# Second MLP product: block sums kept unscaled in accumulators, and operands made for two feature pairs at once

## The chip, the cores and the metric

The kernel runs on one core of a Trainium2 chip. The core has TensorE (matrix products; PE in the profile, its weight loads PEld), VectorE (DVE), ScalarE (ACT), GpSimd (POOL), and SyncE (SP), which issues every transfer of this kernel. Products land in PSUM, everything else lies in SBUF; GpSimd's instructions here read and write SBUF alone. The metric is device microseconds of one execution, lower is better.

## The reference, cut to what matters

Two layers work on 128 context tokens and 1024 grid tokens of 1024 features. Each layer mixes tokens (not touched here) and then applies an MLP with 4096 hidden features:

```
h2 = rms_norm(x, norm2) * (1 + sc2) + sh2
x  = x + g2 * (square(relu(h2 @ w1)) @ w2)
```

`g2`, the gate, has one value per feature and condition; grid and context tokens have different conditions. After the first layer the next one norms x again and projects it; after the second, `rms_norm(x, norm_f)` is the output. The change concerns `@ w2`, the gate and the addition to x.

## The kernel before

**Layout.** Features lie on partitions, tokens along the free dimension: 1152 tokens, in three chunks of 384 for norms and projections, and in four blocks of 288 for the MLP. A block is a quarter of the grid tokens (256) and of the context tokens (32). `hd` in DRAM holds the squared hidden activations.

**Precision.** Each operand is split into two float32r parts: ScalarE rounds a copy (`acopy`, line 181), and a subtraction gives the rest, on GpSimd (`psub`, line 184) or VectorE (`vsub`, line 187). Each product is then three matmuls (lines 1081 to 1083).

**The second product.** Eight groups of four hidden tiles (512 features) follow each other; group g adds its part to all outputs. Within a group, for each of four pairs of output tiles (m) and each half of the tokens (q), a 2 by 2 product of blocks is done with seven products instead of eight (`Line.products`, line 1055 on). That is 4 x 2 x 7 x 2 x 3 = 336 matmuls of 288 columns a group. Such a set of seven for one m and q is called a line below. It ends in four blocks of sums in PSUM (bank names bA, bB, bC), plus a fifth product (bE) that is summed in `z` and added only in the last group.

**What VectorE does for it.** `second` takes each block out of PSUM: `x = gate * sums + x` (line 205), cut by `pieces` where a block crosses a chunk or changes condition: 2, 3, 2 and 2 pieces for the four blocks. x lies in SBUF for the whole product, loaded at its start by 24 transfers. `hidden_operands` (line 1218) makes the seven right operands for a pair of hidden tiles: four `vsub` of 288 columns in place (tile `xb`), seven rounded copies on ScalarE, and seven subtractions (tiles B and T), three on VectorE, four on GpSimd. It is called twice for each half of the tokens. `Weights` makes the left operands: per m and group four sums of 256 columns on VectorE (tile `wl`), seven rounded copies and seven subtractions (tile `wt`); `W2_SUBS` says how many of the seven are on VectorE (two for the first three m, then none).

**What sets the order.** A scheduler puts each engine's instructions in one order by priorities and its own costs, and pools of buffers add waits. The engines run their lists in that order. Within the last group, lines go by halves: all m for the first half of the tokens, then all m for the second. The norm of chunk 0 (`rms_sums`, `rms_rest`) and, in the first layer, its modulation for the next one (`modulate`) are written in between. After the last line come chunks 1 and 2. The next layer's first four projections (`xa`, `gel`) start from chunk 0.

Of the kernel before, what the change touches and what calls it, by code (L numbers as in the profile page):

```python
# [42 lines left out]
# a block of tokens: a quarter of the grid and one of the context  # L43
# [7 lines left out]
W1_SUBS, W2_SUBS = (2, 8, 2, 5), (2, 3)  # L51
# [47 lines left out]
def steps(n, span, i):  # L99
    """How many of n steps fall on i when they are spread over a span."""  # L100
# [17 lines left out]
def build(ctx, tc, I, O):  # L118
# [9 lines left out]
    def urgent(gen, offset):  # L128
        """A stream whose instructions go before those around it."""
# [7 lines left out]
    # pools that come and go  # L137
# [20 lines left out]
    def phase(st, tag, bufs, w=NW, side="left"):  # L158
        """A pool of [128, w] tiles for one phase of a layer."""
# [3 lines left out]
    def two_phases(st, tag, n1, n2, w):  # L163
        """The same in two places, by turns n1 and n2 tiles."""
# [72 lines left out]
    # the early columns apart from the others, which come later  # L237
# [18 lines left out]
    # adaLN vectors, feature on partitions: mod[l][:, j, cond]  # L256
# [3 lines left out]
    def mod_tile(l, j, piece):  # L260
        """mod[l][:, j] from the rows of w_mod's transpose, in pieces."""
# [19 lines left out]
    def segs(n):  # L281
        # (lo, hi, cond) within chunk n
# [4 lines left out]
    def rms_sums(xs, n, alone=False):  # L287
        """The sums over the feature tiles of the squares of chunk n."""
# [14 lines left out]
    def rms_scale(sq, ps, w=P):  # L303
        """1/rms of 3w tokens, to be turned."""
# [11 lines left out]
    def rms_turn(R, ps, w=P):  # L316
        """1/rms of 3w tokens on all partitions, in SBUF."""
# [16 lines left out]
    class HT:  # L334
        """Normalised and modulated activations in two float32r parts, [k][n]."""
# [49 lines left out]
    def weight(src):  # L385
        """The float32r parts of a [128, 8, 128] weight tile, as functions of its k."""
# [17 lines left out]
    def project_tokens(l, group, ht, evac, s_):  # L404
        """256 features projected with the tokens on partitions, 128 tokens a step."""
# [16 lines left out]
    def store_mix(t, dst, n, g_):  # L422
        """The float32r parts of a chunk of 128 features of the mixers' output, to DRAM."""
# [7 lines left out]
    class B:  # L431
        """The arrays of one pair of heads, in chunks of 384 tokens."""
# [243 lines left out]
    def hgrns(pairs):  # L676
        """Both pairs of heads: the end of each part runs under the levels of the next."""
# [10 lines left out]
    RG_STEPS = 1 + 2 * 7  # L688

    def rglru(l, i, xa, gel, gw, ud, g_):  # L690
# [13 lines left out]
        # each function of ScalarE for both directions at once  # L704
# [53 lines left out]
    def split_q(ps, n, h_t, l_t, sub):  # L758
        # queries in the order (row half, column block, row, column) and scaled
# [20 lines left out]
    def qk_project(l, p, win, ht, qd, kd, s_, ns=range(NCH)):  # L780
# [9 lines left out]
        def evac_k(n, ps):  # L790
            # the grid's rows in pairs, by columns
# [12 lines left out]
    # the grid's upper half for all pairs of heads, then the context's tokens and the lower half  # L804
# [4 lines left out]
    # where the output projection is done, by the tokens' half: of the first features, of the last  # L809
# [177 lines left out]
    class Ends:  # L987
        """What becomes of the fifth product and of the four blocks of a product of blocks."""
# [66 lines left out]
    class Line:  # L1055
        """Products of blocks one after the other, the end of each under the start of the next."""
# [53 lines left out]
    def pieces(b):  # L1110
        """Block b of tokens by chunks and conditions: (chunk, from, to, condition, place in the block)."""
# [4 lines left out]
    def half_of(q, t, d, load):  # L1116
        """Moves blocks 2q and 2q + 1 of a [128, 2 * BLK] tile from or to DRAM."""
# [5 lines left out]
    def pair_of(new, name):  # L1123
        return new(name, F32R).rearrange("p (j c) -> p j c", j=2)

    def parts(new, name, t, sub):
        o = pair_of(new, name)
        acopy(o[:, 0], t)
        sub(o[:, 1], t, o[:, 0])
        return o  # L1130

    def load_blocks(srcs, q, new):
        """Blocks 2q and 2q + 1 of two tiles of features."""
        x = []
        for s in srcs:
            t = new("xb")
            if t.shape[1] == 2 * BLK:
                dma(t, s[:, 2 * q * BLK:2 * (q + 1) * BLK])
                x.append((t[:, :BLK], t[:, BLK:]))
            else:  # L1140
                x.append((t[:, :BLK], new("xb")[:, :BLK]))
                for c in range(2):
                    dma(x[-1][c], s[:, (2 * q + c) * BLK:(2 * q + c + 1) * BLK])
        return x
# [22 lines left out]
    class NormOperands:  # L1167
        """The right operands of the seven products, from the features 2i and 2i + 1 of half q of the tokens.

        The steps take 2, 4, 4 and 4 places of [128, 2, BLK] (the second after the first, the fourth after the  # L1170
        others).
        """
# [12 lines left out]
        def normed(self, k):  # L1185
            """Normalised and modulated in place."""
# [31 lines left out]
    def hidden_operands(hd, g, q, i, new_x, new):  # L1218
        """The right operands of the seven products, from the hidden features 2i and 2i + 1 of group g."""
# [687 lines left out]
```

## Time and profile before

| | |
|---|---|
| times of three runs | 3359.71, 3369.78, 3373.78 us; median 3369.78 |
| the profiled execution | span 3359.0 us; its own time is not listed apart, the nearest run is 0.7 us above the span |
| busy shares of the span | PE 89%, PEld 84%, DVE 78%, POOL 52%, ACT 46% |
| second product, layer 0 | first matmul at 1293.7 us, last at 1745 us |
| second product, layer 1 | first matmul at 2886.5 us, last at 3329 us |
| after it, layer 1 | 30 us to the end of the span |

The profile's times are microseconds from the start of the span. A windows row gives, for a stretch, each engine's busy time and in brackets its instructions; then the mean clock that was granted to TensorE (1.00 is full speed), the busy share of the DMA engines and GB/s. A group row (lines) gives the line of the code, engine, operation, output and inputs by name, shape and count, then busy time and the mean nanoseconds of one instruction, then idle time before them and what ended it. Instructions on VectorE overlap a little: the next starts before the one before has written all, so the distance from start to start is shorter than the duration.

### The profile page before, as it was taken

To read this page: it belongs to the slowest core of one execution; us is meant where nothing else is said; L and a number is where in the kernel's file an instruction comes from. 1 tells how busy PE (TensorE), PEld (TensorE's weight loads), DVE (VectorE), ACT (ScalarE), POOL (GpSimd) and SP (SyncE) were. 2 spreads that over 40 slices of the span, in tenths; PEclk is the share of its full clock that TensorE was granted. 3 is DMA by queue.
4 is the path that set the end of the run, shared out by engine and by line. 5 is a ranking of instruction groups with operands and counts; after the bars stand their busy time and mean duration, and the time that the engine had idled before them with its cause. 6 is when DMAs were issued, how large, how long until landed. Compare 5 with 4: busy or idle time off the path is not lost. (4 is left out here: it accounts for less than half of the span.)

```text
span 3359.0 us, 62376 instructions
## 1 busy us (share of the span) xinstructions
PE 2987.9 (89%) x21196; PEld 2829.2 (84%) x21196; DVE 2627.3 (78%) x6417; ACT 1535.1 (46%) x3878; POOL 1735.7 (52%) x1822
## 2 busy tenths in 40 slices
PE   7888998898788888898878899999988999899885
PEld 7877987797788888898878789988878999888885
DVE  7799964678999998999996687345878324899997
ACT  5453234554432225554555533455635333555445
POOL 4541222444744437777765311334546555777776
PEclk8999999999899989999999999999989999999997
DMA  7332449973355555322232212689644333532222
GB/s 269 83 115 89 135 117 272 262 244 114 116 164 159 154 163 171 96 85 89 73 117 67 57 31 78 185 245 289 193 130 122 109 105 106 166 98 86 89 73 73
DMA packets 391070, 452.26 MB, mean 135 GB/s; under 512 B 68192, under 2 KB 293600, under 8 KB 390752
## 3 DMA queue, kind: packets, MB, share of 16 engines
q1 hardware_dynamic: 390752, 448.28, 44.5%
q8 instruction: 168, 2.75, 0.3%
q14 instruction: 150, 1.23, 0.1%
HBM read 339.34 MB, written 108.79 MB: 133 GB/s over the span
## 5 line engine op out<-in xcount | busy, mean ns | idle before, releaser
L184 POOL TENSOR_TENSOR wl<-wr,wh 128x512 fp32r<-128x512 f32 x164 | 226.8, 1388 | 476.6 <-ACT wh L181 380.2
L184 POOL TENSOR_TENSOR ws<-wl,ws 128x512 fp32r<-128x512 f32 x160 | 230.6, 1445 | 231.6 <-ACT ws L181 223.5
L1081 PE MATMUL bB<-t,ws 128*128 128x288 f32 x768 | 240.6, 313 | 73.0 <-DVE hr L193 68.3
L1081 PE MATMUL bB<-T,wt 128*128 128x288 f32 x768 | 240.8, 314 | 67.7 <-ACT bB L181 51.0
L184 POOL TENSOR_TENSOR wt<-wl,wt 128x256 fp32r<-128x256 f32 x296 | 253.0, 862 | 68.7 <-ACT wt L181 65.3
L392 PE MATMUL pj<-hh,wh 128*128 128x384 f32 x640 | 221.5, 351 | 21.4 <-DVE vb L178 7.3
L1082 PE MATMUL bB<-t,ws 128*128 128x288 f32 x768 | 236.3, 308 | 1.0 <-DVE t L187 1.0
L1083 PE MATMUL bB<-t,ws 128*128 128x288 f32 x768 | 236.6, 308 | 0.0
L270 DVE CUSTOM_DVE_ANT_0 junk<-wm,sil,ma 128x384 bf16<-128x384 f32 (+1 forms) x320 | 230.0, 719 | 6.7 <-DMA wm<-in_w_mod 1.9
L1082 PE MATMUL bB<-T,wt 128*128 128x288 f32 x768 | 233.9, 305 | 0.0
L1083 PE MATMUL bB<-T,wt 128*128 128x288 f32 x768 | 232.9, 303 | 0.0
L394 PE MATMUL pj<-hh,wl 128*128 128x384 f32 x640 | 222.4, 348 | 4.2 <-POOL wl L184 4.2
L393 PE MATMUL pj<-hh,wh 128*128 128x384 f32 x640 | 222.9, 349 | 3.4 <-DVE hh L205 3.4
L1081 PEld LDWEIGHTS bB<-t,ws 128*128 128x128 f32 x768 | 153.5, 200 | 81.1 <-DVE hr L193 74.8
L1081 PEld LDWEIGHTS bB<-T,wt 128*128 128x128 f32 x768 | 150.5, 196 | 82.0 <-ACT bB L181 60.6
L184 POOL TENSOR_TENSOR wt<-wr,wt 128x256 fp32r<-128x256 f32 x210 | 184.4, 881 | 60.8 <-ACT wt L181 52.2
L184 POOL TENSOR_TENSOR T<-xb,T 128x288 fp32r<-128x288 f32 x192 | 180.6, 950 | 42.7 <-ACT T L181 42.1
L187 DVE TENSOR_TENSOR xb<-xb 128x288 f32<-128x288 f32 x288 | 190.8, 667 | 11.5 <-POOL B L184 6.3
L181 ACT CAST ws<-wl 128x512 fp32r<-128x512 f32 x160 | 98.7, 620 | 194.8 <-PE bB L1083 91.2
L181 ACT CAST T<-xb 128x288 fp32r<-128x288 f32 x256 | 110.3, 432 | 165.8 <-DVE xb L187 147.3
L1081 PE MATMUL bA<-B,wt 128*128 128x288 f32 x512 | 158.6, 310 | 26.7 <-DVE x L205 23.7
L205 DVE SCALAR_TENSOR_TENSOR x<-bB,mod,x 128x256 f32<-128x256 f32 (+2 forms) x576 | 169.7, 339 | 12.5 <-PE bB L1083 11.5
(336 smaller groups left out, 11474.7 us busy)
## 6 DMA issues: line engine op xcount, KB each, us to landing
wr<-in_w SPq DMA_DIRECT2D x308, 256.0 KB, 3.0
hd<-hr SPq DMA_DIRECT2D x256, 144.0 KB, 2.6
wm<-in_w_mod SPq DMA_DIRECT2D x160, 192.0 KB, 2.7
wr<-in_w_in SPq DMA_DIRECT2D x104, 256.0 KB, 3.1
bi<-in_bias SPq DMA_DIRECT2D x96, 192.0 KB, 4.3
QS<-qd SPq DMA_DIRECT2D x72, 256.0 KB, 4.2
xb<-hd SPq DMA_DIRECT2D x128, 144.0 KB, 2.2
xb<-hd SPq DMA_DIRECT2D x64, 288.0 KB, 2.8
```

The costliest lines, as they stand in the source:

```text
L181: nc.scalar.copy(out=out, in_=in_)
L184: nc.gpsimd.tensor_tensor(out=out, in0=a, in1=b, op=ALU.subtract)
L187: nc.vector.tensor_tensor(out=out, in0=a, in1=b, op=ALU.subtract)
L205: nc.vector.scalar_tensor_tensor(out=out, in0=a, scalar=s, in1=b, op0=op0, op1=op1)
L270: nc.vector.tensor_tensor_reduce(out=junk[:, :w], in0=r[:, :w], in1=sil[:, c, k0:k0 + w], scale=1.0, scalar=acc[c], op0=ALU.mult, op1=ALU. ...
L392: mm(ps, lhsT=wh(k), rhs=ah(k), start=k == first, stop=False)
L393: mm(ps, lhsT=wh(k), rhs=al(k), start=False, stop=False)
L394: mm(ps, lhsT=wl(k), rhs=ah(k), start=False, stop=k == last)
L1081: mm(ps, lhsT=w[:, 0, ti(i)], rhs=t[:, 0], start=start and i == 0, stop=False, skip_group_check=True)
L1082: mm(ps, lhsT=w[:, 0, ti(i)], rhs=t[:, 1], start=False, stop=False, skip_group_check=True)
L1083: mm(ps, lhsT=w[:, 1, ti(i)], rhs=t[:, 0], start=False, stop=i == n - 1, skip_group_check=True)
```

## The change

1. The sums of a block go to an accumulator `acc` of 288 columns per block and output tile, without gate and without x. In group 0 ScalarE copies them out of PSUM; in the other seven, one VectorE addition per block. `z` is added to `acc` in the same way in the last group.
2. x is not loaded at the start. Where a chunk is complete, its eight x tiles are loaded (`load_chunk`) and `combine` does `x = gate * acc + x` on SBUF data: six pieces per output tile for all three chunks, 48 instructions a layer.
3. `hidden_operands` makes operands of both pairs at once: all its instructions are 576 columns wide, half as many. Its input tiles hold both pairs; there are two for all halves.
4. `W2_SUBS` becomes (4, 3, 2): four of seven subtractions of the left operands on VectorE for the first three m, then two.
5. At the end of layer 0, chunks 1 and 2 are loaded once the pools of the second product are closed, and both are modulated before the next layer's projections are written; before, chunk 2 was modulated after the projections of chunk 0.

Its core:

```diff
-W1_SUBS, W2_SUBS = (2, 8, 2, 5), (2, 3)
+W1_SUBS, W2_SUBS = (2, 8, 2, 5), (4, 3, 2)
+HIDDEN_SUBS = (0, 0, 1, 0, 0, 1, 1)
...
-    def hidden_operands(hd, g, q, i, new_x, new):
-        (a1, b1), (a2, b2) = load_blocks([hd[GRP * g + k] for k in (2 * i, 2 * i + 1)], q, new_x)
-        subs = iter((psub, psub, psub, vsub, psub, vsub, vsub))
+    def hidden_operands(hd, g, q, new_x, new):
+        src = hd[GRP * g:GRP * (g + 1)].rearrange("(i two) p t -> two p i t", two=2)
+        x = []
+        for s in range(2):
+            t = new_x("xb")
+            dma(t.rearrange("p (i t) -> p i t", i=2), src[s][:, :, 2 * q * BLK:2 * (q + 1) * BLK])
+            t = t.rearrange("p (i c m) -> p i c m", i=2, c=2)
+            x.append((t[:, :, 0], t[:, :, 1]))
+        (a1, b1), (a2, b2) = x
+        subs = iter(HIDDEN_SUBS)
+
+        def parts(name, t):
+            o = new(name, F32R).rearrange("p (j i m) -> p j i m", j=2, i=2)
+            acopy(o[:, 0], t)
+            (vsub if next(subs) else psub)(o[:, 1], t, o[:, 0])
+            return o
...
             def add(k, c, ps):
-                for n, a, b, cc, o in pieces(2 * q + c):
-                    t = xs[k][n][:, a:b]
-                    vstt(t, ps[:, o:o + b - a], mod[l][:, 40 + k, cc:cc + 1], t, ALU.mult, ALU.add)
+                t = acc[k][:, 2 * q + c]
+                if g == 0:
+                    acopy(t, ps)
+                else:
+                    vtt(t, ps, t, ALU.add)
...
+        def load_chunk(n):
+            for k in range(KD):
+                xs[k][n] = new_x("xo")
+                dma(xs[k][n], xmid[k][:, cs(n)])
+
+        def combine(n):
+            for k in range(KD):
+                t = xs[k][n]
+                g = mod[l][:, 40 + k]
+                for b in range(4):
+                    for nn, a, e, cc, o in pieces(b):
+                        if nn == n and cc == 0:
+                            vstt(t[:, a:e], acc[k][:, b, o:o + e - a], g[:, 0:1], t[:, a:e], ALU.mult, ALU.add)
+                if n == NCH - 1:
+                    u = t[:, NW - TP:].rearrange("p (b c) -> p b c", b=4)
+                    vstt(u, acc[k][:, :, BLG:], g[:, 1:2], u, ALU.mult, ALU.add)
...
             for n in range(NCH):
                 for m, e in first:
                     run_out(project(win(m), ht, e, (n,)))
-                if n == 0:
-                    modulate(l, False, xs, 2, ht)
```

**On VectorE, in the middle of layer 0's second product.** Twelve rows before (x is the residual, xb, B and T the right operands, wl the sums of weights):

```order
L187 TENSOR_TENSOR B_19406<-xb,B_19406 128x288
L193 TENSOR_TENSOR wl<-wr 128x256
L187 TENSOR_TENSOR xb<-xb 128x288
L187 TENSOR_TENSOR wl<-wl,wr 128x256
L187 TENSOR_TENSOR T_19416<-xb,T_19416 128x288
L205 SCALAR_TENSOR_TENSOR x_15501<-bA,mod_116,x_15501 128x256
L205 SCALAR_TENSOR_TENSOR x_15505<-bA,mod_116,x_15505 128x32
L205 SCALAR_TENSOR_TENSOR x_15503<-bA,mod_116,x_15503 128x256
L205 SCALAR_TENSOR_TENSOR x_15505<-bA,mod_116,x_15505 128x32
L205 SCALAR_TENSOR_TENSOR x_15507<-bB,mod_116,x_15507 128x128
L205 SCALAR_TENSOR_TENSOR x_15509<-bB,mod_116,x_15509 128x128
L205 SCALAR_TENSOR_TENSOR x_15511<-bB,mod_116,x_15511 128x32
```

and twelve after, from the same part of the product (acc is the accumulator, wt a part of a left operand):

```order
L188 TENSOR_TENSOR xb<-xb 128x2x288
L194 TENSOR_TENSOR acc<-bA,acc 128x288
L194 TENSOR_TENSOR z_16009<-bE,z_16009 128x288
L188 TENSOR_TENSOR xb<-xb 128x2x288
L194 TENSOR_TENSOR wl<-wr 128x256
L188 TENSOR_TENSOR wt<-wr,wt 128x256
L194 TENSOR_TENSOR acc<-bB,acc 128x288
L194 TENSOR_TENSOR acc<-bC,acc 128x288
L188 TENSOR_TENSOR wl<-wl,wr 128x256
L194 TENSOR_TENSOR acc<-bA,acc 128x288
L194 TENSOR_TENSOR acc<-bB,acc 128x288 x2
L188 TENSOR_TENSOR xb<-xb 128x2x288
```

Two or three instructions per block of sums have become one, the operands are twice as wide, and subtractions of weights (wt) now stand on VectorE.

**On ScalarE, where layer 1's first projections leave PSUM** (pj is the projection's bank, xa and gel its targets, sq squares for a norm, hh and hm modulated chunks). Before:

```order
L208 ACTIVATE hh_21185<-nt,mod_117 128x384
L208 ACTIVATE hh_21190<-nt,mod_117 128x384
L208 ACTIVATE sq<-x_15533 128x384
L181 CAST wh<-wr 128x512
L181 COPY xa<-pj 128x384
L181 CAST wh<-wr 128x512
L208 ACT_TABLE_LOAD
L208 ACTIVATE gel<-pj 128x384
```

After:

```order
L209 ACTIVATE hh_20657<-nt,mod_117 128x256
L209 ACTIVATE hh_20657<-nt,mod_117 128x128
L209 ACTIVATE hh_20665<-nt,mod_117 128x256
L209 ACTIVATE hh_20665<-nt,mod_117 128x128
L182 COPY xa<-pj 128x384 x2
L182 CAST wh<-wr 128x512 x2
L209 ACTIVATE gel<-pj 128x384
L182 CAST wh<-wr 128x512 x2
```

The first copy of `xa` stood between the norms of chunks 0 and 1; now it stands behind the last modulated tile of chunk 2 (hh_20665, in pieces of 256 and 128).

## Rows read from the trace of the kernel before

**Rows 1.** Windows: length, then busy us (xinstructions) of PE, PEld, DVE, ACT, POOL; PEclk, DMA.
```profile
1293.00:1340.00 47.00, 38.85 (x242) 35.67 (x243) 46.05 (x91) 27.16 (x81) 40.26 (x46) 0.93 0.65 210
1340.00:1653.00 313.00, 279.94 (x2003) 272.98 (x2003) 294.75 (x752) 157.62 (x437) 232.43 (x268) 0.97 0.29 88
1653.00:1745.00 92.00, 75.17 (x491) 71.92 (x489) 90.44 (x217) 47.30 (x118) 63.78 (x73) 0.93 0.28 95
1745.00:1800.00 55.00, 45.20 (x242) 43.17 (x241) 38.92 (x68) 30.44 (x64) 31.44 (x23) 0.91 0.29 96
2650.00:2850.00 200.00, 200.00 (x1510) 200.00 (x1510) 65.73 (x118) 72.32 (x156) 107.21 (x96) 1.00 0.34 103
```

**Rows 2.** Waits of TensorE, 1340 to 1653 us (total us, times, longest).
```profile
PE bB L1081 <- ACT bB L181: 21.9, 15, 4.0
```

**Rows 3.** VectorE's groups of instructions, 1340 to 1653 us (busy us, mean ns).
```profile
L187 DVE TENSOR_TENSOR xb<-xb 128x288 f32<-128x288 f32 x102 | 64.7, 639 | 4.2 <-POOL B L184 2.4 <-POOL T L184 1.7
L187 DVE TENSOR_TENSOR B<-xb,B 128x288 fp32r<-128x288 f32 x50 | 36.1, 732 | 2.5 <-ACT B L181 2.5
L187 DVE TENSOR_TENSOR T<-xb,T 128x288 fp32r<-128x288 f32 x25 | 14.5, 580 | 0.2 <-ACT T L181 0.2
L193 DVE TENSOR_TENSOR z<-bE,z 128x288 f32<-128x288 f32 x48 | 21.2, 445 | 0.3 <-PE bE L1083 0.3
L187 DVE TENSOR_TENSOR wl<-wr 128x256 f32<-128x256 f32 x24 | 18.8, 784 | 0.2
L187 DVE TENSOR_TENSOR wl<-wl,wr 128x256 f32<-128x256 f32 x23 | 13.8, 601 | 0.0
```

**Rows 4.** VectorE in order of time (start us, duration, line, instruction, count).
```profile
1665.47 0.63 DVE L205 SCALAR_TENSOR_TENSOR x<-bA,mod,x 128x256 f32<-128x256 f32 x2
1666.02 0.41 DVE L187 TENSOR_TENSOR wl<-wl,wr 128x256 f32<-128x256 f32 x1
1667.03 0.75 DVE L205 SCALAR_TENSOR_TENSOR x<-bC,mod,x 128x128 f32<-128x128 f32 x3
1667.70 0.44 DVE L187 TENSOR_TENSOR xb<-xb 128x288 f32<-128x288 f32 x1
1668.07 0.44 DVE L187 TENSOR_TENSOR B<-xb,B 128x288 fp32r<-128x288 f32 x1
...
1691.43 0.54 DVE L193 TENSOR_TENSOR sq<-sq 128x384 f32<-128x384 f32 x1
1691.89 0.41 DVE L187 TENSOR_TENSOR wl<-wr 128x256 f32<-128x256 f32 x1
```

**Rows 5.** VectorE while GpSimd works, in order of time.
```profile
1298.22 0.98 DVE L187 TENSOR_TENSOR T<-xb,T 128x288 fp32r<-128x288 f32 x1
1299.12 0.95 DVE L187 TENSOR_TENSOR wt<-wr,wt 128x256 fp32r<-128x256 f32 x1
1299.99 0.96 DVE L187 TENSOR_TENSOR wl<-wr 128x256 f32<-128x256 f32 x1
```

**Rows 6.** GpSimd in the same microseconds.
```profile
1297.94 1.85 POOL L184 TENSOR_TENSOR wt<-wl,wt 128x256 fp32r<-128x256 f32 x2
```

**Rows 7.** GpSimd's groups of instructions, 1340 to 1653 us.
```profile
L184 POOL TENSOR_TENSOR wt<-wl,wt 128x256 fp32r<-128x256 f32 x96 | 82.2, 861 | 27.5 <-ACT wt L181 27.4
L184 POOL TENSOR_TENSOR T<-xb,T 128x288 fp32r<-128x288 f32 x76 | 71.2, 946 | 14.0 <-ACT T L181 13.8
```

**Rows 8.** VectorE's groups of instructions, 1653 to 1745 us: the sums' last additions.
```profile
L205 DVE SCALAR_TENSOR_TENSOR x<-z,mod,x 128x32 f32<-128x32 f32 x16 | 10.6, 660 | 0.0
L205 DVE SCALAR_TENSOR_TENSOR x<-z,mod,x 128x128 f32<-128x128 f32 x16 | 9.8, 653 | 0.0
L205 DVE SCALAR_TENSOR_TENSOR x<-z,mod,x 128x256 f32<-128x256 f32 x8 | 5.9, 734 | 0.0
```

**Rows 9.** Waits of TensorE where layer 0 ends, 1720 to 1840 us.
```profile
PE pj L393 <- DVE hm L205: 4.8, 1, 4.8
```

**Rows 10.** VectorE's last instructions for the norm of the third chunk.
```profile
1788.84 2.06 DVE L205 SCALAR_TENSOR_TENSOR hh<-nt,mod,hh 128x256 fp32r<-128x256 f32 x6
```

More of the change, by code (lines that the diff above doesn't have):

```diff
@@ L1121, in half_of @@
             dma(*((a, d_) if load else (d_, a)))
[L1123 to L1144, printed above, removed]
     def blocks_of(t):
@@ L1704, in build @@
             sil_st.close()
-        x_st, h_st = ExitStack(), ExitStack()
-        X = x_st.enter_context(tc.tile_pool(name="x", bufs=24, side="right", reuse_waits="tile"))
-        st0, st1 = ExitStack(), ExitStack()
-        hr_ = phase(st0, "hr", 2, 2 * BLK, "right")
-        tp = [two_phases(st0, "tp0", 12, 2, 2 * BLK)]
+        h_st, acc_st, st0, st1, xs_st = (ExitStack() for _ in range(5))
+        acc_ = phase(acc_st, "acc", KD, T, "right")
+        hr_ = phase(st0, "hr", 2, 4 * BLK, "right")
+        tp = [two_phases(st0, "tp0", 6, 1, 4 * BLK)]
         ring2 = phase(st0, "wt", W2_RING, 4 * P, "right")
-        z_ = phase(st0, "z5", 8, BLK, "right")
-        tp += [two_phases(st1, "tp1", 11, 3, 2 * BLK), phase(st1, "tp2", 14, 2 * BLK, "right")]
+        z_ = phase(st0, "z5", 4, BLK, "right")
+        tp += [two_phases(st1, "tp1", 5, 2, 4 * BLK), phase(st1, "tp2", 7, 4 * BLK, "right")]
         def group_operands(s):
-            return [hidden_operands(hd, s // 2, s % 2, i, sqt if i % 2 else hr_, tp[s % 3]) for i in range(2)]
+            return hidden_operands(hd, s // 2, s % 2, hr_, tp[s % 3])
         ops = {s: group_operands(s) for s in range(2)}
-        xs = [[None] * NCH for _ in range(KD)]
-        for m in range(KD):
-            for n in range(NCH):
-                xs[m][n] = xt(f"x{m}")
-                dma(xs[m][n], xmid[m][:, cs(n)])
+        acc = [acc_("acc").rearrange("p (b m) -> p b m", b=4) for _ in range(KD)]
         z = [[None] * 2 for _ in range(KD // 2)]
@@ L1726, in build @@
         weights = Weights([I["w2"][l, g, m] for g in range(NG) for m, _ in order[g]], 2, lambda: ring2("wt", F32R), W2_RING,
-                          lambda i: lo_subs(W2_SUBS[0] if i < W2_SUBS[1] else 0))
+                          lambda i: lo_subs(W2_SUBS[0] if i < W2_SUBS[1] else W2_SUBS[2]))
         line = Line(banks, weights)
@@ L1746, in second @@
             return Ends(p5, *(lambda ps, r=r, c=c: add(2 * m + r, c, ps) for r in range(2) for c in range(2)))
-        def norm_part(n, k=KD):
-            pass
+        def load_chunk(n):
[13 more added lines that the diff above has]
+                    vstt(u, acc[k][:, :, BLG:], g[:, 1:2], u, ALU.mult, ALU.add)
         if not last:
             xold = tc.dram_tile([KD, P, T], F32, name=f"xd{l}")
+        xs = [[None] * NCH for _ in range(KD)]
         v = 0
@@ L1756, in build @@
                 for q in qs:
-                    line.add(v, q == qs[-1], lambda p, i, t=ops[2 * g + q]: t[i][p], 2, second(g, m, q))
+                    line.add(v, q == qs[-1], lambda p, i, t=ops[2 * g + q]: t[p][:, :, i], 2, second(g, m, q))
                     if g < NG - 1 and (m, q) in ((1, 1), (KD // 2 - 1, 1)):
@@ L1766, in build @@
                         ht = HT(8)
+                    new_x = phase(xs_st, "xo", (NCH if last else 1) * KD, NW, "right")
+                    load_chunk(0)
+                    combine(0)
                     sq = rms_sums(xs, 0)
@@ L1772, in build @@
                         finish(xs, 0, rs)
+                        for n in (1, 2):
+                            load_chunk(n)
                     else:
@@ L1777, in build @@
         line.end()
-        st0.close()
-        if last:
-            for n in (1, 2):
-                finish(xs, n, rms_chunk(xs, n, pa))
-            x_st.close()
-        else:
+        if not last:
+            xs_st.close()
+            st0.close()
+            new_x = phase(xs_st, "xo", 2 * KD, NW, "right")
+            with tc.high_priority(URGE2):
+                for n in (1, 2):
+                    load_chunk(n)
             ph = ExitStack()
             ht.open(ph)
-            for n in (1, 2):
+        for n in (1, 2):
+            combine(n)
+            if last:
+                finish(xs, n, rms_chunk(xs, n, pa))
+            else:
                 for m in range(KD):
                     dma(xold[m][:, cs(n)], xs[m][n])
-            modulate(l + 1, False, xs, 1, ht)
+                modulate(l + 1, False, xs, n, ht)
+        xs_st.close()
+        st0.close()
+        acc_st.close()
+        if not last:
+            x_st = ExitStack()
+            X = x_st.enter_context(tc.tile_pool(name="x", bufs=24, side="right", reuse_waits="tile"))
 def host_inputs(inp):
```

16 lines of the change are left out of this document (8 added, 8 removed).

## The prediction

> **What bounds the kernel now.** I read the page's busy shares first, then windows over the second product, then the waits of TensorE in its middle, then groups and the order of time on VectorE and GpSimd. The middle of layer 0's second product, 1340 to 1653 us, holds 2003 matmuls [rows 1]; a group has 336, so these are six groups (a few records are missing) of 313 / 6 = 52.2 us. VectorE is busy 294.75 us of the 313, 49.1 us a group. TensorE could be faster: where VectorE is busy a third of the time (65.73 of 200 us in layer 1's first product), it does 1510 matmuls in 200 us [rows 1], 0.1325 us each, 44.5 us for 336. What holds it back is seen in its waits: the largest, 21.9 us, is for ScalarE's copy from bA to bB [rows 2], whose bank must first be emptied by VectorE. So the stage runs at VectorE's pace, with 6% on top (52.2 / 49.1). What the change is worth is what it takes from VectorE, as far as TensorE's 44.5 us.
>
> **Part 1: sums leave PSUM unscaled.** Of the four blocks, three come out in two pieces and one in three; a group has eight of each kind. Two pieces take 0.55 us from start to start (1665.47 to 1666.02), three take 0.67 (1667.03 to 1667.70) [rows 4]. A group: 24 x 0.55 + 8 x 0.67 = 18.6 us. The new addition is that of z: 288 columns, one input in PSUM, 0.445 us [rows 3], less 0.07 that the next instruction overlaps (0.44 against 0.37 from start to start, 1667.70 to 1668.07 [rows 4]): 0.375. 32 x 0.375 = 12.0. Saved: 6.6 us a group.
>
> **Part 2: operands of double width.** 28 instructions of 288 columns a group become 14 of 576. The row at 288 goes from start to start in 0.37, that at 384 in 0.46 (1691.43 to 1691.89) [rows 4]: 0.94 ns a column, and 0.10 us that does not depend on width. Merging saves 14 x 0.10 = 1.4 us. [...]
>
> **Part 3: weight subtractions move to VectorE.** Two of seven for each of four m: 8 a group. Free of GpSimd, 256 columns take 0.41 - 0.07 = 0.34 us [rows 4]; where GpSimd works all along (two subtractions in 1.85 us from 1297.94 [rows 6]), the same kind takes 0.87 from start to start (1299.12 to 1299.99 [rows 5]). That bounds the eight between 2.7 and 7.0 us. Over the middle, sums of the same width take 0.60 to 0.78 [rows 3], about 0.69 - 0.07 = 0.62; I take that: 5.0 us more.
>
> **Part 4: less collision with GpSimd.** VectorE's instructions with both inputs in SBUF are slowed by GpSimd; those from PSUM are not (z: 0.445 on average in the same stretch [rows 3]). The excess over 0.44 is 0.20 for xb, 0.29 for B and 0.14 for T, 0.21 on average over 177; over 0.41 it is 0.28 for wl [rows 3]. A group carries 28 x 0.21 + 16 x 0.28 = 10.4 us of excess, and with the eight new ones 12.6. GpSimd is busy 232.43 / 6 = 38.7 us of 52.2, 74% [rows 1]. It loses eight subtractions of 0.86 us [rows 7], 7 us: 31.7 of some 47.5 us, 67%. I count nothing for its merged instructions. If the excess goes with that share, it falls to 11.4: 1.2 us saved.
>
> **The middle.** 49.1 - 6.6 - 1.4 + 5.0 - 1.2 = 44.9 us of VectorE a group, and TensorE needs 44.5. Two engines that both need about 45 us and wait for each other will not both be full; with the 6% of before I come to 47.5. That is 4.7 us a group; for the fourteen groups after each layer's first, 66 us.
>
> **First groups.** Layer 0's first 47 us hold 242 matmuls, and VectorE is busy for 46.05 of them [rows 1]. The rest of the group at the middle's pace makes 61 us. All 18.6 us of additions go from VectorE to ScalarE, which is busy 27.16 of the 47 us [rows 1] and so has room for 32 copies; the 24 loads of x go too. Against that stand more weight subtractions, and only two input tiles: the second half's hidden activations can't be loaded before the first half's operands are made. I take 6 us saved for each layer, 12 in all (0 if the input tiles decide, 15 if VectorE does).
>
> **Last groups and layer ends.** z is added in 40 pieces that take 10.6 + 9.8 + 5.9 = 26.3 us [rows 8], 23 with the overlap; 16 additions of 288 columns at the xb row's 0.64 [rows 3] take 9. Chunk 0's combine adds sixteen instructions at the same rows' 0.73 (256 columns) and 0.65 (128) [rows 8], 10 us. Saved: 4 us a layer. Chunks 1 and 2 add 32 more, 20 us at those durations, 11 at the free ones (0.55 us for the pair of 256 and 128, from rows 4's slope). In layer 1 they stand before the last sums in VectorE's order, in a stretch where VectorE has no room: I take 12 us, net 8 lost. In layer 0 the price is in ScalarE's order: the first copy of xa now comes behind chunk 2's last modulated tile. Before, that tile was done at 1788.84 + 2.06 = 1790.9 us [rows 10], 46 us after the last sums, with TensorE busy 45.2 of 55 us on projections [rows 1] and one long wait of 4.8 us [rows 9]. Now the banks of the first projections stay full until then, so TensorE can do about three of twelve projections and then waits. The same norm chain with 11 us of combine in it, but without waiting for a projection, should end about as late; three projections of 72 matmuls of 384 columns (0.177 us each by columns from 0.1325) fill 24 x 3 x 0.177 = 13 us, or more if they wait for chunk 0 as before. I take 8 us more idle time (0 to 20). Net for layer 0: 4 lost.
>
> **The sum.** -66 - 12 + 8 + 4 = -66 us, from the profiled span of 3359.0: 3293. The median of the runs is 10.8 us above that span and the nearest run 0.7; I add 7 and forecast 3300 us.
>
> **The rivals.**
> - TensorE's floor. If what VectorE loses takes its waits away altogether, a group takes 45.5 us, 6.7 less, 94 in fourteen: 3359 - 94 - 12 + 12 + 7 = 3272. For it: layer 1's first product runs without gaps at a third of VectorE's load. Against: here VectorE still has 45 us of work.
> - A chain takes VectorE's place. Instructions twice as wide come later, the two input tiles serve every half, and an addition from PSUM may stand behind a subtraction of 1.1 us or more. A group then takes 50.0 us: 31 us saved, nothing in the first groups, 12 lost at the ends: 3359 - 31 + 12 + 7 = 3347. For it: the 6% of gaps exist already [rows 1]. Against: operands are made about one half ahead.
> - Slower: the collision grows. With eight more instructions on VectorE that read SBUF twice, and longer ones on both engines, each could meet GpSimd more often. All at the slowed rate (0.90 for 288 columns, 1298.22 to 1299.12, 0.87 for 256 [rows 5]), 14 x 1.80 + 24 x 0.87 = 46 us, where my sum has 28.5; half of that difference makes 54 us of VectorE and 55 of span, 2.8 us more a group. 3359 + 39 + 12 + 7 = 3417. It decides from 4.2 us of added excess on, where VectorE is back at 49.1. [...] Against the rival: GpSimd's work shrinks by 7 us a group.
> - That the change does not do what it says is excluded by the order: 32 additions in place of 72 pieces stand there.
>
> **How the numbers follow.** Forecast 0.53, own range 3275 to 3325. TensorE's floor 0.15, the chain 0.22, the collision 0.10. The 0.5% that a measurement can tell is 17 us, so faster means below 3353: the forecast, the floor and half of the chain, 0.79. The other half of the chain and the collision's mild end make no change, 0.12. Slower, 0.09. The range runs from 3252 (the floor with 20 us more) to 3358 (the chain's upper end); the collision lies outside.
>
> **What would show it.** In the middle's windows, some 350 matmuls in 50 us in place of 320, VectorE still busy nine tenths or more, and GpSimd at two thirds. The additions into acc at 0.44 to 0.45 us; the double-width ones between 0.7 and 1.3 on average; wt on VectorE at 0.6 to 0.75. A shorter wait of bB for ScalarE. At the end of layer 0 one wait of TensorE of 10 to 25 us that ends with a copy of xa. I am wrong if wt on VectorE or the wide ones come near twice their free time, if a group takes 50 us or more, or if the first group takes as long as before.

## The result, and the profile after

The changed kernel takes 3390.11 us (median of six runs, 3375.41 to 3401.95) against 3366.85 us before (six runs, 3359.71 to 3373.78). The ratio is 1.0063, 95% interval 1.0039 to 1.0087: slower by 0.4 to 0.9%, where 3300 us had been forecast. The profiled execution has a span of 3389.7 us, before 3359.0; the one before is near the fastest of its runs, so this difference of 30.7 us is 7 us larger than that of the medians (23.3).

Where the 30.7 us arise can be read from the matmuls of the second product, counted in order: 336 are a group, and a group lasts from its first matmul's start to that of the next group, the last one to the start of the layer's last matmul. "Between" is the time from layer 0's last such matmul to layer 1's first; the two numbers are those of the layers.

| part | before | after | difference | forecast |
|---|---|---|---|---|
| first groups | 65.4, 63.4 | 70.4, 68.0 | +9.6 | -12 |
| groups 2 to 7, mean | 51.9 | 49.8 | 12 x -2.15 = -25.8 | 12 x -4.7 = -56.4 |
| last groups | 74.6, 67.3 | 78.1, 75.6 | +11.8 | -5.4 |
| between | 1141.6 | 1174.6 | +33.0 | +8 |
| start and end | 1293.7, 30.0 | 1293.9, 31.9 | +2.1 | 0 |

The stretches of [rows 1], in the changed kernel:

```profile
1293.00:1340.00 47.00, 37.15 (x204) 33.85 (x205) 37.20 (x48) 29.94 (x82) 31.64 (x28) 0.78 0.32 100
1340.00:1653.00 313.00, 291.07 (x2092) 282.96 (x2091) 263.87 (x473) 160.10 (x385) 191.57 (x179) 0.98 0.30 92
1653.00:1745.00 92.00, 72.94 (x456) 66.75 (x454) 86.68 (x174) 43.12 (x105) 48.92 (x49) 0.93 0.43 140
1745.00:1800.00 55.00, 21.70 (x87) 20.55 (x87) 32.41 (x73) 21.61 (x47) 13.43 (x10) 0.60 0.14 49
2650.00:2850.00 200.00, 200.00 (x1510) 200.00 (x1509) 59.57 (x114) 70.77 (x153) 105.95 (x95) 1.00 0.35 104
```

The middle (second row) does 2092 matmuls in place of 2003, with VectorE busy 84% of the time (before 94%) and GpSimd 61% (74%). The first 47 us do 204 in place of 242, at a clock of 0.78. From 1745 us on there are 87 in place of 242, at 0.60.

What TensorE waits for in the middle, to be held against [rows 2]:

```profile
PE bB L1082 <- ACT bB L182: 15.7, 15, 3.6
PE bB L1082 <- ACT bC L182: 3.4, 4, 0.9
PE bA L1082 <- DVE acc L194: 1.3, 2, 0.8
```

VectorE's groups there, to be held against [rows 3]:

```profile
L188 DVE TENSOR_TENSOR xb<-xb 128x576 f32<-128x576 f32 x53 | 58.2, 1099 | 3.6 <-POOL B L185 2.4 <-POOL T L185 0.7 <-DMA xb<-hd 0.2
L194 DVE TENSOR_TENSOR acc<-bB,acc 128x288 f32<-128x288 f32 x91 | 40.9, 449 | 24.2 <-PE bB L1084 23.9
L188 DVE TENSOR_TENSOR wt<-wr,wt 128x256 fp32r<-128x256 f32 x50 | 31.2, 624 | 8.0 <-ACT wt L182 7.9
L188 DVE TENSOR_TENSOR T<-xb,T 128x576 fp32r<-128x576 f32 x26 | 22.1, 849 | 3.3 <-ACT T L182 3.1
L188 DVE TENSOR_TENSOR B<-xb,B 128x576 fp32r<-128x576 f32 x13 | 17.5, 1343 | 2.2 <-ACT B L182 2.2
```

The durations are the forecast ones. New is the idle time: VectorE stands 23.9 us ahead of additions whose sums TensorE hasn't finished, while TensorE stands 15.7 us for a copy behind such additions. They wait for each other by turns.

And TensorE's waits at the end of layer 0, where [rows 9] had one of 4.8 us:

```profile
1753.18 0.69 PE L393 MATMUL pj<-hh,wh 128*128 128x384 f32 x1 [8.02 <-ACT gel L209]
1762.26 1.47 PE L321 MATMUL rb<-ident,dg 128*128 128x128 f32 x6 [1.28 <-DVE dg L179]
1775.24 1.44 PE L308 MATMUL st<-few,sq 128*128 128x2 f32 x6 [11.52 <-DVE sq L194]
1778.94 1.65 PE L321 MATMUL rb<-ident,dg 128*128 128x128 f32 x6 [2.26 <-DVE dg L179]
1790.81 0.69 PE L393 MATMUL pj<-hh,wh 128*128 128x384 f32 x1 [10.22 <-ACT xa L182]
```

In brackets stands how long TensorE had waited, and for what. These add up to 33 us of standing still in 46 (1745 to 1791 us).

### The profile page after: what moved, and what is told of

Read it like the earlier page. It is cut to its first block, busy times and chain, and to the rows that moved or that the text cites. A ratio compares the mean times of both kernels' runs of the same rounds, so it can differ in the third digit from the quotient of the medians.

```text
span 3389.7 us, 60910 instructions
## 1 busy us (share of the span) xinstructions
PE 2991.3 (88%) x21196; PEld 2826.1 (83%) x21196; DVE 2522.0 (74%) x5685; ACT 1527.5 (45%) x3716; POOL 1592.6 (47%) x1546
## 5 line engine op out<-in xcount | busy, mean ns | idle before, releaser
L185 POOL TENSOR_TENSOR wt<-wl,wt 128x256 fp32r<-128x256 f32 x284 | 259.1, 922 | 93.8 <-ACT wt L182 69.6
L393 PE MATMUL pj<-hh,wh 128*128 128x384 f32 x640 | 223.9, 354 | 44.4 <-ACT xa L182 10.2
L1082 PEld LDWEIGHTS bB<-t,ws 128*128 128x128 f32 x768 | 152.1, 198 | 76.8 <-DVE hr L194 71.1
L393 PE MATMUL wo<-u,wh 128*128 128x288 f32 x512 | 157.9, 310 | 22.0 <-DVE x L206 10.1
L188 DVE TENSOR_TENSOR xb<-xb 128x576 f32<-128x576 f32 (+1 forms) x160 | 164.5, 1029 | 11.9 <-POOL B L185 8.7
L393 PEld LDWEIGHTS pj<-hh,wh 128*128 128x128 f32 x640 | 125.8, 198 | 50.3 <-ACT xa L182 10.5
L203 POOL TENSOR_SCALAR pl<-pl,rc 128x384 f32<-128x384 f32 x128 | 78.6, 614 | 189.8 <-DVE rc L924 67.7
L191 POOL TENSOR_TENSOR hr<-hr 128x288 f32<-128x288 f32 x128 | 108.7, 855 | 119.0 <-ACT hr L209 116.6
```

The costliest lines, as they stand in the source:

```text
L185: nc.gpsimd.tensor_tensor(out=out, in0=a, in1=b, op=ALU.subtract)
L188: nc.vector.tensor_tensor(out=out, in0=a, in1=b, op=ALU.subtract)
L191: nc.gpsimd.tensor_tensor(out=out, in0=a, in1=b, op=op)
L203: nc.gpsimd.tensor_scalar(out=out, in0=a, scalar1=s1, scalar2=s2, op0=op0, op1=op1)
L393: mm(ps, lhsT=wh(k), rhs=ah(k), start=k == first, stop=False)
L1082: mm(ps, lhsT=w[:, 0, ti(i)], rhs=t[:, 0], start=start and i == 0, stop=False, skip_group_check=True)
```

## The experiments

All ratios are to the kernel before, with 95% intervals. Each kernel was measured beside it; its medians in those later series are 3362.9 to 3365.1 us, so a ratio can't be worked out from this table's first row. Groups and "between" are counted as above, from each kernel's profiled execution, one for each. How far one execution can be trusted is seen in `xa_early` and `no_combine`, which have the same code up to layer 1's last group: their first groups agree within 1.0 us and their middles within 0.1, but layer 0's last groups differ by 5.4 us and "between" by 3.8. `light_adds`, `light_pool`, `light_xb` and `no_combine` leave out a part of the computation, to see what it costs.

| kernel | us | ratio | first groups | middle, mean | last groups | between |
|---|---|---|---|---|---|---|
| before | 3366.85 | | 65.4, 63.4 | 51.9 | 74.6, 67.3 | 1141.6 |
| after | 3390.11 | 1.0063 (1.0039 to 1.0087) | 70.4, 68.0 | 49.8 | 78.1, 75.6 | 1174.6 |
| xa_early | 3364.79 | 1.0000 (0.9988 to 1.0012) | 69.9, 68.6 | 49.7 | 75.6, 75.7 | 1153.3 |
| narrow | 3400.66 | 1.0098 (1.0079 to 1.0118) | 60.6, 62.8 | 51.6 | 73.9, 76.1 | 1181.7 |
| old_subs | 3382.63 | 1.0056 (1.0034 to 1.0078) | 71.1, 71.7 | 49.1 | 74.2, 75.1 | 1173.9 |
| light_adds | 3399.14 | 1.0096 (1.0077 to 1.0115) | 70.1, 68.3 | 50.8 | 76.6, 75.0 | 1173.5 |
| light_pool | 3254.31, one run | | 54.5, 56.9 | 44.8 | 61.7, 67.5 | 1154.3 |
| light_xb | 3361.78, one run | | 69.6, 68.5 | 49.1 | 78.3, 75.3 | 1152.3 |
| sums_only | 3361.75, one run | | 60.6, 60.8 | 50.7 | 70.3, 77.9 | 1156.2 |
| no_combine | 3363.94, one run | | 70.5, 67.6 | 49.8 | 81.0, 67.4 | 1157.1 |
| hidden_pool | 3345.40 | 0.9952 (0.9933 to 0.9970) | 67.6, 70.1 | 48.7 | 79.4, 77.7 | 1144.0 |
| hybrid | 3364.09 | 0.9995 (0.9986 to 1.0005) | 71.2, 69.5 | 49.5 | 80.7, 75.0 | 1148.4 |
| inputs4 | 3354.66 | 0.9970 (0.9958 to 0.9982) | 66.2, 66.1 | 49.5 | 78.1, 76.1 | 1154.4 |
| first_both | 3351.99 | 0.9968 (0.9955 to 0.9981) | 68.4, 67.6 | 49.2 | 78.2, 76.8 | 1146.4 |
| place | 3352.59 | 0.9973 (0.9962 to 0.9984) | 57.3, 60.6 | 49.9 | 80.5, 76.6 | 1155.3 |
| best1 | 3337.15 | 0.9922 (0.9907 to 0.9938) | 67.1, 66.7 | 48.3 | 77.0, 76.9 | 1150.9 |
| best2 | 3336.06 | 0.9917 (0.9901 to 0.9933) | 66.3, 66.2 | 47.8 | 79.1, 74.6 | 1145.3 |
| best3 | 3339.75 | 0.9932 (0.9915 to 0.9949) | 68.2, 67.7 | 47.7 | 77.3, 78.3 | 1151.3 |
| best4 | 3338.73 | 0.9927 (0.9906 to 0.9948) | 62.9, 61.6 | 47.6 | 77.8, 78.2 | 1157.2 |

**The end of layer 0.** `xa_early`, on the changed kernel:

```diff
-                xa[i][n] = g_("xa")
+                xa[i][n] = xt("xa") if l else g_("xa")
```

> The changed kernel with one line different: in layer 1 the tiles of the first projections (xa) come from the pool of the long-lived chunk tiles (x) and no longer from the mixer's own pool, which lies over the tiles of chunks 1 and 2 of x and opens only when these are free. In ScalarE's order the first copy of xa then stands before chunk 1's norm and no longer behind chunk 2's last modulated tile. Theory 1 (TensorE stood at the end of layer 0 because the banks of its first projections could not be emptied): the waits of 11.5 us for the norm's sums and of 10.2 us for xa go, TensorE's clock does not stay low for 34 us from 1762 us on, and layer 1's second product starts 20 to 28 us earlier than in the changed kernel (2914.6 us); the whole time falls by as much, to about 3363 us in runs whose changed kernel has 3390. Theory 2 (the late sums and combines of chunks 1 and 2 on VectorE hold TensorE, whatever the order of xa): another wait takes their place, less than 8 us gained.

"Between" fell by 21.3 us and the loss was gone. TensorE's largest waits from 1720 to 1840 us became these:

```profile
PE pj L393 <- ACT xa L182: 7.2, 2, 6.6
PE pj L395 <- POOL wl L185: 4.5, 2, 3.4
PE gr L712 <- DVE xc L206: 3.8, 2, 2.2
PE pj L393 <- ACT hm L209: 3.6, 1, 3.6
```

The two waits of more than 10 us are gone, so theory 1 holds. Of the 33.0 us between the layers, 11.7 stay; the wait of 6.6 us may be part of them, the rest was not taken apart.

**The middle: how much VectorE has to do.** `light_adds`, on the changed kernel, and `light_pool`, on `xa_early`:

```diff
-                    vtt(t, ps, t, ALU.add)
+                    w = 32 if g < NG - 1 else BLK; vtt(t[:, :w], ps[:, :w], t[:, :w], ALU.add)
```

> The changed kernel with the additions into acc in groups 1 to 6 done on 32 of 288 columns only (the other columns' sums are left out); every wait stays, each addition is shorter by some 0.27 us, 8 to 9 us of VectorE a group. Theory 1 (VectorE's time sets the pace): groups fall from 49.6 us to 46 or less. Theory 2 (the chain of banks does, through its order and fixed times): each hand-over is 0.27 us shorter, but groups fall by 1 us at most.

```diff
-            (vsub if next(subs) else psub)(o[:, 1], t, o[:, 0])
-            return o
+            if next(subs):
+                vsub(o[:, 1], t, o[:, 0])
+                return o
+            psub(o[:, 1, :, :16], t[:, :, :16], o[:, 0, :, :16])
+            return First(o)
```

`First` gives part 0 where part 1 is asked for; the weights' subtractions on GpSimd are cut in the same way.

> The kernel with the early xa, with GpSimd's subtractions in the second product done on 32 columns only (TensorE reads the rounded part in place of the rest there, so the small parts of these operands are left out). GpSimd loses three quarters of its work there, VectorE keeps every instruction and every place in its order, and the instructions of VectorE from SBUF should come down to their free times (0.41 to 0.45, 0.7 at 576 columns). VectorE's load falls from some 42 to 35 us a group, as it did with the light additions, which brought nothing. Theory 1 (TensorE waits where a run of SBUF instructions stands between two additions in VectorE's order, and the collision stretches that run): the waits of bB for ScalarE shrink by more than half, and a group falls from 49.5 to 47.5 or less. Theory 2 (the bank chain's own order and times set the pace): 49 or more.

The fourth group of layer 0 in both, as windows, `light_adds` first:

```profile
1464.20:1513.30 49.10, 45.34 (x338) 44.84 (x337) 34.49 (x79) 24.28 (x58) 30.28 (x29) 1.00 0.29 92
```

```profile
1431.90:1476.60 44.70, 44.70 (x338) 44.70 (x337) 34.27 (x78) 24.96 (x58) 10.65 (x28) 1.00 0.31 100
```

VectorE is busy 34.5 and 34.3 us, on 79 and 78 instructions, at the same granted clock. With the one the group takes 49.1 us (50.8 over all twelve, a us more than without the cut, at a granted clock of 0.97 in place of 1.00 in the third to seventh groups), with the other TensorE has no gap at all and needs 44.7, near the 44.5 forecast as its floor. So it isn't VectorE's load that sets the pace. What does can be seen in the changed kernel at 1482 us, on VectorE:

```profile
1482.10 0.44 DVE L194 TENSOR_TENSOR acc<-bB,acc 128x288 f32<-128x288 f32 x1
1482.46 1.58 DVE L188 TENSOR_TENSOR xb<-xb 128x576 f32<-128x576 f32 x1
1483.97 0.96 DVE L188 TENSOR_TENSOR wt<-wr,wt 128x256 fp32r<-128x256 f32 x1
1484.86 0.45 DVE L194 TENSOR_TENSOR z<-bE,z 128x288 f32<-128x288 f32 x1
1485.22 0.58 DVE L188 TENSOR_TENSOR wl<-wr 128x256 f32<-128x256 f32 x1
1485.72 0.95 DVE L188 TENSOR_TENSOR wl<-wr,wl 128x256 f32<-128x256 f32 x1
1486.60 0.74 DVE L188 TENSOR_TENSOR T<-xb,T 128x576 fp32r<-128x576 f32 x1
1487.27 0.45 DVE L194 TENSOR_TENSOR acc<-bB,acc 128x288 f32<-128x288 f32 x1
```

on ScalarE:

```profile
1487.75 0.38 ACT L182 COPY bB<-bA 128x288 f32<-128x288 f32 x1 [2.08 <-DVE acc L194]
```

and on TensorE:

```profile
1488.18 0.40 PE L1082 MATMUL bB<-T,wt 128*128 128x288 f32 x1 [0.61 <-ACT bB L182]
```

Between two additions that free a bank bB stand six other instructions. They take 4.8 us (1482.46 to 1487.27), stretched by GpSimd: xb takes 1.58 us here, and on average 0.76 in `light_pool`:

```profile
L188 DVE TENSOR_TENSOR xb<-xb 128x576 f32<-128x576 f32 x44 | 33.2, 759 | 8.0 <-POOL T L185 3.4 <-DMA xb<-hd 2.4 <-POOL B L185 1.7
```

ScalarE's copy waits 2.1 us for the second addition, and TensorE for the copy. A shorter addition doesn't shorten the run ahead of it. In `light_pool`, with GpSimd busy some 10 us a group in place of 30, the run fits under TensorE's other banks: one wait for bB is left in 283 us:

```profile
PE bB L1093 <- ACT bB L182: 0.5, 1, 0.5
```

GpSimd's load can act by its collision with VectorE or by late operands, and `light_pool` takes away both. Against late operands stands that no wait of TensorE in the changed kernel's middle ends with GpSimd; `hidden_pool` below is the stronger test.

`light_xb`, on `xa_early`, should have shortened the runs alone; all four subtractions in place are cut alike:

```diff
+        w = 36 if 0 < g < NG - 1 else BLK
+        xsub = lambda o, a, b: vsub(o[:, :, :w], a[:, :, :w], b[:, :, :w])
...
-        vsub(a1, b1, a1)
+        xsub(a1, b1, a1)
```

> Early xa, with the four wide subtractions in place (xb) of each half done on 72 of 576 columns in groups 1 to 6 (the other columns' combinations are left out): eight instructions a group shorter by some 0.9 us each, 7 us of VectorE, as much as the light additions took away. If the runs of SBUF instructions between two additions set the pace, a group falls from 49.5 to 48 or less, where the light additions left it at 50.6. If neither load nor runs matter but the bank chain's fixed times, it stays at 49 or more.

```profile
L188 DVE TENSOR_TENSOR xb<-xb 128x72 f32<-128x72 f32 x40 | 25.4, 634 | 2.5 <-DMA xb<-hd 1.7 <-POOL B L185 0.6
```

An eighth of the columns still takes 634 ns (1085 for the whole in `xa_early`), so the edit took away 8 x 0.45 = 3.6 us a group, half of what it should. Groups are at 49.1 us, by the letter on the side of the other theory (49 or more), but with so little taken away the run decides nothing. What it shows is that next to GpSimd most of what such an instruction takes is not work on its columns: by [rows 4] (0.44 us for 288 columns, 0.94 ns a column) 72 columns would take some 0.24 us undisturbed, an estimate, and 0.63 were measured. How GpSimd stretches it was not shown. In `light_adds`, with GpSimd as busy (30.3 us in the fourth group, here 28.5), 32 columns of an addition from PSUM into acc took 186 ns.

**The middle: the parts of the change.** `old_subs` is the changed kernel with `W2_SUBS = (2, 3, 0)`, `narrow` the changed kernel with the old `hidden_operands`, and `sums_only` has both of these edits and that of `xa_early`.

> The changed kernel with the weights' subtractions where they were: two of seven on VectorE for the first three m, then none, so that VectorE has eight fewer a group and GpSimd eight more. Theory 1 (VectorE's load still sets the pace): VectorE loses some 4 to 5 us a group and a group falls from 49.6 to about 47. Theory 2 (the handing over of banks between TensorE, VectorE and ScalarE sets it, at any load of VectorE below some 44 us): within 0.5 us of 49.6. Theory 3 (GpSimd is needed soon): GpSimd back at 40 us a group, and groups grow to 51 or more with waits of TensorE for wt.

> The changed kernel with the right operands made as before: 288 columns per instruction, one pair of hidden tiles at a time, input tiles as before. Sums, combine, subtractions of weights and the end of layer 0 stay changed. Theory 1 (the wide operands and their two input tiles make the first operands of a product late): the first groups fall from 70.4 and 68.0 us to 62 to 65, and the clock is low there for about 14 us in place of 24 to 27. Theory 2 (the 32 copies on ScalarE in group 0 make them late): they stay at 68 or more. For the middle (49.6 us a group): if instructions of more than 1 us standing ahead of the additions make TensorE wait, a group falls to 48 or less; if VectorE's load does, it grows by about the 1.4 us that the merging saved, to 51; if neither, it stays.

> Only the sums of the change: accumulators and late combine, operands of 288 columns as before, subtractions of weights as before, early xa. VectorE has 6.6 us a group less to do than in the kernel before. If its load set the pace before, a group is at 46 to 48 (52 before). If the bank chain behind runs of SBUF instructions did already, the groups stay at 50 to 52, and this part of the change alone brings next to nothing in the middle.

In old_subs theory 2 held, but it is a weak test: VectorE's busy time fell by only 0.9 us a group (from 42.0 to 41.1 in layer 0's third to seventh groups), though eight subtractions of 0.624 us, 5.0 us, had left it; so its other instructions took some 4 us a group longer, an estimate from these numbers. In narrow theory 1 held for the first groups, and the middle grew by 1.8 us, near the theory that VectorE's load counts; light_adds speaks against that one. The sums alone brought 1.3 us a group (51.9 to 50.7), not 6.6; the weights' subtractions on VectorE cost 0.7 (49.1 to 49.8); the wide operands bring the most, 1.8 (51.6 to 49.8), though a part of that is the granted clock (in `narrow` 0.97 to 0.98 in the third to seventh groups, after 1.00).

`hidden_pool`, on `xa_early`, takes three wide instructions out of VectorE's order for each half of the tokens:

```diff
-HIDDEN_SUBS = (0, 0, 1, 0, 0, 1, 1)
+HIDDEN_SUBS = (0, 0, 0, 0, 0, 0, 0)
```

> The kernel with the early xa, with all seven subtractions of the right operands on GpSimd (three of them were on VectorE), 576 columns each: six fewer a group on VectorE, six more on GpSimd. If runs of wide instructions between two additions make TensorE wait, groups fall from 49.5 to 48 to 48.5. If GpSimd, then at 42 us or more of some 49, makes the operands late, groups grow to 51 or more, with waits of TensorE for GpSimd's B and T, and the first groups grow too.

From the third group on it has 46.5 to 48.0 us, as expected if the runs count. GpSimd's cost is where the other theory put it: in the second groups, 53.1 and 55.3 us. The fourth group of layer 0, `xa_early` first:

```profile
1458.40:1507.20 48.80, 46.28 (x339) 44.90 (x338) 41.96 (x80) 24.41 (x58) 30.00 (x29) 1.00 0.29 93
```

```profile
1457.30:1505.00 47.70, 45.26 (x338) 44.79 (x337) 42.36 (x72) 24.87 (x58) 37.83 (x35) 1.00 0.30 95
```

The group is shorter although VectorE (the third figure after the length) is busy as long and GpSimd (the fifth) 7.8 us longer. So neither engine's load alone sets the pace; what changed in the group's favour is that fewer instructions stand between the additions in VectorE's order (72 in place of 80 in all).

**The first groups.** Three edits on `xa_early`: `hybrid` makes group 0's operands in two steps of 288 columns, `inputs4` gives them two more input tiles, `first_both` does both.

```diff
-            return hidden_operands(hd, s // 2, s % 2, hr_, tp[s % 3])
+            return hidden_operands(hd, s // 2, s % 2, acc_ if s == 1 else hr_, tp[s % 3])
```

> The kernel with the early xa, and in group 0 of each second product the right operands made in two steps of 288 columns, the first pair of hidden tiles and then the second, in the same wide tiles; groups 1 to 7 stay at 576. If the wide instructions make the first operands late, the first groups (69.9 and 68.6 us) fall to 61 to 64, as with narrow operands throughout (60.6 and 62.8), the other groups stay at 49.5, and the whole time falls by 12 to 16 us against the kernel with early xa (3364.8), to about 3350. If the two input tiles are what makes them late, the first groups stay above 67.

> The kernel with the early xa, with two more input tiles for the second half of the tokens of group 0: they are taken from the pool of acc, whose last two tiles are written late in that group. All operands stay 576 wide. If the second half's loads and operands wait for the first half's input tiles, and that makes the first group slow, the first groups fall from 69.9 and 68.6 us to 60 to 63 and the time by 12 to 18 us, to about 3350. If the wide first operands or the copies on ScalarE make it slow, the groups stay above 67 us.

> Early xa, and in group 0 both: operands in two steps of 288 columns, and two more input tiles for the second half of the tokens. If the first group needs both (small first steps, and inputs that don't wait for one another), it falls from 66 (more tiles alone) and 70 (small steps alone) to 60 to 62, as with the narrow operands, and the whole to about 3345. If something else of the narrow operands did it (its order of subtractions between the engines), it stays at 65 or more.

None came near the 60.6 us of `narrow`: 3 us from the tiles, nothing from the steps. Neither the width nor the number of input tiles is the main cause; the traces showed another. ScalarE's first copies of operands of the second product in `narrow`, whose first matmul is at 1292.5 us:

```profile
1273.91 0.43 ACT L182 CAST B<-xb 128x288 fp32r<-128x288 f32 x1 [1.16 <-DMA xb<-hd]
1276.65 0.43 ACT L182 CAST T<-xb 128x288 fp32r<-128x288 f32 x1 [0.20 <-DVE xb L188]
```

and in the changed kernel, first matmul 1293.9:

```profile
1292.91 0.66 ACT L182 CAST B<-xb 128x576 fp32r<-128x576 f32 x1
```

18.6 us ahead there, 1.0 us here. In the kernel before it was 18.7 (first matmul 1293.7):

```profile
1274.99 0.43 ACT L181 CAST B<-xb 128x288 fp32r<-128x288 f32 x1 [1.08 <-DMA xb<-hd]
```

The pool of these tiles has 6 + 1 of double width; the first lies where an operand of the first product is used to its end, and the other operands come from inputs that are changed in place once it is made. `place` moves that one tile:

```diff
-        tp = [two_phases(st0, "tp0", 6, 1, 4 * BLK)]
+        tp = [two_phases(st0, "tp0", 5, 2, 4 * BLK)]
```

> Early xa, and the pool of the first operands split as 5 and 2 tiles in place of 6 and 1: the first operand's tile then lies over operands of the first product's first half, which are free early, and no longer over one that is used to the end. In ScalarE's order the first five operands of the second product then stand among the first product's last lines. Theory 1 (the place of that tile made the first group late): the first rounded operand is made 15 to 19 us before the first matmul of the second product, as in the kernel before (18.7), in place of 1.0, and the first groups fall from 69.9 and 68.6 us to 60 to 64; the whole to about 3350. Theory 2 (wide first operands are slow wherever they lie): 67 us or more.

```profile
1276.26 0.67 ACT L182 CAST B<-xb 128x576 fp32r<-128x576 f32 x1 [0.44 <-DMA xb<-hd]
1280.33 0.68 ACT L182 CAST T<-xb 128x576 fp32r<-128x576 f32 x1 [1.65 <-DVE xb L188]
```

The first copy comes 19.7 us ahead, and the first groups fall by 12.6 and 8.0 us: theory 1. The mean granted clock of layer 0's first group is 0.81 in the changed kernel, 0.91 in `place` (before 0.90), so the late operands cost some clock as well. Part of the gain is given back ahead, since the operands are now made under the first product: its last 62 us hold 375 matmuls, in `xa_early` 400.

**The last groups.** `no_combine`, on `xa_early`: `combine(n)` only where `not last`.

> The kernel with the early xa, without the combine of chunks 1 and 2 of layer 1 (32 instructions of VectorE; gate and product are left out of these chunks, the loads of x stay). If these instructions in the stretch where VectorE is full cost the time at the end, layer 1's last group falls from 75.7 to 67 to 70 us, and the end with it by 8 to 12 us. If the loads of x at that place cost it, less than 3 us.

Layer 1's last group falls from 75.7 to 67.4 us, the price of 32 instructions: 8.3 us, as expected (but for light_pool, the other kernels with these instructions have 74.6 to 78.3 us there). The whole did not fall with it (3363.94 us, one run): layer 0's last group and "between" were 5.4 and 3.8 us longer in this execution.

**A faster version.** `best1` has the edits of `xa_early`, `inputs4` and, from group 1 on, `hidden_pool`; `best2` the last from group 2 on; `best3` adds to `best2` the edit of `hybrid`, `best4` that of `place`.

> Early xa, four input tiles in group 0, and from group 1 on all seven subtractions of the right operands on GpSimd. If the gains add up: first groups 60 to 63, groups 1 to 6 at 47.7 (those of the kernel with all of them on GpSimd), the whole 3325 to 3335. If GpSimd has a backlog after group 0, group 1 is at 53 to 55 again.

> As the kernel before it in this list, with the subtractions on GpSimd from group 2 on. Group 1 some 50 us in place of 53 to 55 where GpSimd was late; groups 2 to 6 at 47.7; the whole 3325 to 3335, within 5 us of the other.

> The fastest kernel so far (3336.1) with the small first steps in group 0 as well. First groups 60 to 62 in place of 66.3 and the whole 3324 to 3328 if the first group needs both; 3336 if not.

> The fastest kernel (3336.1; first groups 66.3) with that split. Theory 1: first groups 58 to 62, the whole 3322 to 3328. Theory 2: no change, 3336.

best1 and best2 beat both kernels, before by 0.6 to 1.0%, though each came 1 to 2 us above the range expected of it. best3 and best4 are no faster than best2. best4 missed its 3322 to 3328 us by 11: its first groups are 3.4 and 4.6 us shorter than best2's, but its first product ends later (second product from 1298.0 us, in best2 from 1288.9) and "between" is 11.9 us longer.

## Why the prediction was wrong

It forecast -66 us from the span and +30.7 came, 96.7 us apart. The failed steps, by size:

1. **The middle (31 us).** Right were the additions' 0.449 us, wt's 0.624, the wide ones' 0.85 to 1.34, GpSimd's smaller share; VectorE's work fell even further than to 44.9 us, to 84% of 49.8 = 42. Its terms were mis-sized, though: in layer 0's third to seventh groups VectorE is busy 49.3 us a group before, 44.9 in `sums_only`, 45.1 in `narrow` and 42.0 after, so the sums took away 4.4 us (6.6 forecast), the weights' subtractions added 0.2 (5.0 less 1.2), and the wide operands took away 3.1 (1.4). What failed for the time is "so the stage runs at VectorE's pace, with 6% on top": the 6% was no constant loss but the mechanism. Already in [rows 2] TensorE's wait ends with a copy that waits for an addition in VectorE's order, and how long the run ahead of that addition is decides: in layer 0's fourth group, VectorE was busy 42.0 us of 48.8 in `xa_early`, 34.5 of 49.1 in `light_adds`, and 42.4 of only 47.7 in `hidden_pool`. The second rival said so ("an addition from PSUM may stand behind a subtraction of 1.1 us or more") and gave 50.0 us a group; it had a chance of 0.22.
2. **The end of layer 0 (27 us, with the end of layer 1).** The mechanism was right: three projections, then a wait for xa behind chunk 2. The size was not: the prediction's own 13 us of work in a stretch of 46 leave 33 us idle, and before it was about 9. I took 8 more, not 24. And the cause lies deeper than ScalarE's order: xa's pool opens only when the tiles of chunk 2's x are free.
3. **The first groups (22 us).** "I take 6 us saved" counted VectorE's and ScalarE's work (and the 61 us it gave layer 0's first group before are 65.4 by count). It wasn't asked where the wider tiles lie and what has to be finished ahead of them; the order shows the first B copy behind the first product's last lines.
4. **The last groups (17 us).** Chunks 1 and 2's combine cost 8.3 us in layer 1, near the 12 taken. What failed is the saving: 4.7 + 4 us a layer didn't come. That VectorE's load isn't the price, as in the middle, is likely, but was not tested here. Layer 0's last group also grew by 3.5, which is within what one execution differs from another.

The rival of growing collision had the right enemy in the wrong way: the mean excess did not grow (wt at 0.62 as forecast), yet with GpSimd's load cut to a third the middle is at TensorE's floor.

## What to carry to other kernels

A busy share of 94% does not make an engine the bound: follow one wait of the waiting engine back, and look at what stands in order ahead of the instruction that ends it. When tiles get wider or change pools, ask for the first user of each new tile what lay in its place and when that is free. And add up idle time from the stretch, work against length, not by feeling.

## What the hardware showed that was not expected

Next to GpSimd, most of what VectorE's subtraction in place (xb, both inputs in SBUF) took did not go with its width: with an eighth of the columns it still took 634 of 1085 ns on average. With GpSimd's work cut, the wide ones (xb and T) took 759 and 761 ns in `light_pool`.

Across the waits at the end of layer 0 the mean granted clock was 0.60 over 55 us (before 0.91). After the waits of 8.0 and 10.2 us the projections' matmuls of 384 columns first started 0.32 us apart, and only later 0.17. So these two waits were paid twice, in idle time and in slower work behind them. In `light_pool`'s fourth group, where TensorE never stood still, the granted clock was 1.00.
